# Layer 0's MLP: the first projection in seven products of quarters per pair of feature tiles

## The chip, the cores and the metric

The kernel runs on one core of a Trainium2 chip. A core has TensorE (PE, the matmuls; its weight loads stand in a row of their own, PEld), VectorE (DVE), ScalarE (ACT), GpSimd (POOL) and SyncE (SP), which here issues all the DMAs. The metric is the device time of one execution in microseconds (us). The kernel before takes 1741.64 us (median of 3 runs, 1736.88 to 1743.53).

## The reference

A block of two layers works on 512 latent tokens and 256 context tokens of width 1024. Each layer is a token mixer (layer 0: gated linear attention, "GLA"; layer 1: neighbourhood attention, "NA") and then a gated MLP with a depthwise convolution of width 3 over the tokens. Each of these four parts starts with an RMS norm that is scaled and shifted by vectors computed from the conditioning input (adaLN: six vectors of 1024 per layer), and ends with a gate and a residual add. What the change touches is the MLP and the adaLN vectors:

```
mod_l = (sc_lat @ ada_w[i] + ada_b[i])[:, None, :]          # six vectors per layer: shift, scale, gate, twice

def conv_ffn(h, w_in, conv_w, conv_b, w_out):               # D_MODEL 1024, D_FF 2816
    a, val = jnp.split(h @ w_in, 2, axis=-1)
    ap = jnp.pad(a, ((0, 0), (1, 1), (0, 0)))
    a = ap[:, :-2] * conv_w[0] + ap[:, 1:-1] * conv_w[1] + ap[:, 2:] * conv_w[2] + conv_b
    return (jax.nn.silu(a) * val) @ w_out
```

In layer 0 the MLP runs on the context tokens too (768 tokens in all), in layer 1 on the 512 latent ones alone. All arithmetic is float32.

## The kernel before, in words

Activations are kept transposed: features on the 128 partitions, tokens along the free axis. `H` holds the normed input of a projection as two float32r tiles, `hh` (the rounded value) and `hl` (what the rounding left); weights are held the same way as `wh` and `wl`. A product of full accuracy is then three matmuls, in `mm3` (L249 `hh` by `wl`, L250 `hl` by `wh`, L251 `hh` by `wh`). The helper `wunit` brings a weight unit of 128x1024: a DMA into `st` (pool `wst`, 3 buffers), an ACT copy into `wh` (L244), a DVE subtraction into `wl` (L245; pool `whl`, 5 buffers of each).

The stages run in this order: start and first norm, GLA, the GLA's output projection with the second norm (`finish_gla`), layer 0's MLP, NA, layer 1's MLP with the final norm. A static scheduler lays out the program: it sets the order of the instructions on each engine when the kernel is built, and each engine then works through its own list strictly in that order, waiting where an operand is late.

Layer 0's MLP has 22 pairs of feature tiles j (a tile of `a` and a tile of `val`, 128 features each), in six groups of three and a last group of four. For each pair, `in_tile` makes four matmul groups of 8 k-blocks x 3 matmuls: for `a` the 512 latent tokens (LAT) and the 256 context tokens (CTX), then the same for `val`. `finish` then does, on one row of 769 columns: ACT copies the `a` results into `apad` (L788), DVE convolves (L822, L823, L824), ACT applies Silu (L825), DVE multiplies by `val` (L830) and splits the result into `uh` and `ul` (L261 ACT, L262 DVE). After a group of three pairs comes the second projection: for each of 8 output tiles and both token ranges, 9 matmuls over the group's three tiles, and a gated add into the residual on DVE (L273). I call the two halves of a group its **in-phase** and its **out-phase**.

Between the pairs, DVE also computes eight adaLN vectors of layer 1 (`ada_lanes`): per vector eight DMAs of 512 KB into `sa` (pool `ast`, 2 buffers) and eight DVE multiply-adds of 128x1024 into `acc` (L201, L203), four steps after each pair; PE then sums over the partitions.

NA works through eight pairs of heads. For one pair, PE projects the next pair's q, k and v, makes scores (L964), transposes the softmax'd scores (`turn`, L989) and multiplies them with v (`values`, L1006). Between them DVE adds the bias and takes the maximum (L971), POOL, ACT and DVE do the softmax, and ACT (L992) and DVE (L994) each copy one head's transposed scores `PT` out of PSUM, which `values` waits for.

## Time and profile before

| | |
|---|---|
| median of 3 runs | 1741.64 us (1736.88 to 1743.53) |
| the profiled execution, its own time | 1739.42 us |
| its span, first to last instruction | 1737.6 us |
| mean granted TensorE clock in it | 0.993 |
| PE, PEld, DVE, ACT, POOL busy | 97%, 81%, 62%, 38%, 11% of the span |
| layer 0's MLP, in the trace | from about 452 us to about 1020 us |
| NA, in the trace | from about 1040 us to about 1345 us |

How to read the views that follow. The page gives the busy time of each engine over the span and the chain of work that ended last. A row that groups instructions reads: line, engine, operation, tile written from tiles read, shapes, count, then busy us in total, mean ns of one, and after the bar the idle time of the engine before them with what ended it. A timeline row reads: start us, duration us, engine, line, operation. A matmul's duration contains the time to run through the array, so that the rows of consecutive matmuls overlap: what a matmul costs is the distance between two starts. A row of stretches reads: stretch, its length, then for each engine busy us and, in brackets, the number of instructions.

### The profile page before, as it was taken

What the parts mean: (1) busy time and instruction counts of PE and PEld (TensorE: products, weight loads), DVE (VectorE), ACT (ScalarE), POOL (GpSimd) and SP (SyncE); (2) the same over time, 40 slices, a digit from 0 to 9 for tenths busy, and PEclk for the clock granted to TensorE, in tenths of its full rate; (3) what the DMA queues carried; (4) which work ended last, traced back from release to release, by engine and by line L of the source; (5) the groups of instructions that cost most, each with busy time, mean ns of one, the idle gap of its engine ahead of it and who ended that gap; (6) DMA issues with size and microseconds to landing.
All of it is one profiled execution on the core that took longest, in us unless ns stands there. A gap on an engine that the chain in (4) does not pass through costs nothing.

```text
span 1737.6 us, 27175 instructions
## 1 busy us (share of the span) xinstructions
PE 1681.7 (97%) x11107; PEld 1413.8 (81%) x11107; DVE 1070.4 (62%) x1699; ACT 658.7 (38%) x1173; POOL 190.9 (11%) x324
## 2 busy tenths in 40 slices
PE   5999999999999999999999999999999999999997
PEld 3767778778888888888888888888888888888887
DVE  4797777977666655656544575445456755555555
ACT  3675655653422121212213264443334522222332
POOL 1031212220000000000000015332222000000000
PEclk9999999999999999999999999999999999999999
DMA  7553423026224543544412122112111233223321
GB/s 274 173 171 122 154 90 104 19 72 220 86 73 152 160 125 110 179 147 146 122 60 86 49 68 79 54 42 66 54 56 42 75 97 98 90 82 95 109 85 49
DMA packets 54188, 179.70 MB, mean 103 GB/s; under 512 B 7024, under 2 KB 10864, under 8 KB 54064
## 3 DMA queue, kind: packets, MB, share of 16 engines
q1 hardware_dynamic: 54064, 177.97, 32.6%
q8 instruction: 87, 1.43, 0.3%
q14 instruction: 37, 0.30, 0.1%
HBM read 173.75 MB, written 2.10 MB: 101 GB/s over the span
## 4 chain that ended last, share of the span: by engine, by line
PE 80%; DVE 10%; ACT 4%; DMA 2%; issue 2%; POOL 1%; SPq 0%; POOLq 0%; DVEq 0%; ACTq 0%
PE mm L249 18%; PE mm L251 17%; PE mm L250 17%; PE aux L249 6%; PE aux L250 6%; PE aux L251 6%; PE mm L1006 2%; DMA sa<-in 2%; PE aux L989 2%; PE aux L964 2%; DVE t L526 1%; PE aux L605 1%; PE aux L570 1%; DVE acc L203 1%; DVE t L525 1%
## 5 line engine op out<-in xcount | busy, mean ns | idle before, releaser
L249 PE MATMUL mm<-hh,wl 128*128 128x512 f32 (+3 forms) x1104 | 388.6, 354 | 3.9 <-ACT hh L329 2.5
L251 PE MATMUL mm<-hh,wh 128*128 128x512 f32 (+3 forms) x1104 | 383.3, 348 | 0.0
L250 PE MATMUL mm<-hl,wh 128*128 128x512 f32 (+3 forms) x1104 | 383.0, 347 | 0.0
L244 ACT ACTIVATE wh<-st 128x1024 fp32r<-128x1024 f32 (+1 forms) x189 | 196.2, 1052 | 314.1 <-PE mm L251 162.4
L245 DVE TENSOR_TENSOR wl<-st,wh 128x1024 fp32r<-128x1024 f32 (+1 forms) x188 | 229.1, 1228 | 32.3 <-ACT wh L244 31.7
L249 PEld LDWEIGHTS mm<-hh,wl 128*128 128x128 f32 (+1 forms) x1104 | 208.8, 190 | 35.8 <-issue 5.5
L250 PEld LDWEIGHTS mm<-hl,wh 128*128 128x128 f32 (+1 forms) x1104 | 209.4, 190 | 24.3 <-issue 0.8
L251 PEld LDWEIGHTS mm<-hh,wh 128*128 128x128 f32 (+1 forms) x1104 | 209.1, 189 | 24.4 <-issue 0.4
L249 PE MATMUL aux<-hh,wl 128*128 128x512 f32 (+2 forms) x576 | 201.1, 349 | 0.0
L250 PE MATMUL aux<-hl,wh 128*128 128x512 f32 (+2 forms) x576 | 201.0, 349 | 0.0
L251 PE MATMUL aux<-hh,wh 128*128 128x512 f32 (+2 forms) x576 | 200.8, 349 | 0.0
L249 PE MATMUL mm<-uh,wl 128*128 128x512 f32 (+1 forms) x560 | 194.1, 350 | 1.7 <-ACT uh L261 1.4
L250 PE MATMUL mm<-ul,wh 128*128 128x512 f32 (+1 forms) x560 | 194.2, 348 | 0.0
L251 PE MATMUL mm<-uh,wh 128*128 128x512 f32 (+1 forms) x560 | 193.3, 346 | 0.0
L273 DVE SCALAR_TENSOR_TENSOR xl<-mm,mod,xl 128x512 f32<-128x512 f32 (+1 forms) x168 | 116.3, 698 | 108.9 <-PE mm L251 108.6
L305 POOL TENSOR_TENSOR rs<-ms,mhalf 128x2 f32<-128x2 f32 (+1 forms) x10 | 11.6, 1160 | 1036.6 <-DVE ms L303 1036.6
L249 PEld LDWEIGHTS mm<-uh,wl 128*128 128x128 f32 x560 | 105.8, 190 | 20.0 <-ACT uh L261 3.7
L249 PEld LDWEIGHTS aux<-hh,wl 128*128 128x128 f32 x576 | 109.2, 190 | 15.0 <-issue 1.4
L250 PEld LDWEIGHTS aux<-hl,wh 128*128 128x128 f32 x576 | 109.2, 190 | 14.4 <-issue 1.1
L251 PEld LDWEIGHTS aux<-hh,wh 128*128 128x128 f32 x576 | 109.1, 189 | 14.0 <-issue 0.8
L250 PEld LDWEIGHTS mm<-ul,wh 128*128 128x128 f32 x560 | 106.4, 190 | 14.3 <-DVE ul L262 0.3
L251 PEld LDWEIGHTS mm<-uh,wh 128*128 128x128 f32 x560 | 106.2, 190 | 13.1
(207 smaller groups left out, 2462.4 us busy)
## 6 DMA issues: line engine op xcount, KB each, us to landing
st<-in SPq DMA_DIRECT2D x201, 512.0 KB, 3.7
sa<-in SPq DMA_DIRECT2D x98, 512.0 KB, 4.3
sx<-in SPq DMA_DIRECT2D x14, 512.0 KB, 5.7
xl<-in SPq DMA_DIRECT2D x8, 512.0 KB, 5.6
xc<-in SPq DMA_DIRECT2D x4, 512.0 KB, 7.8
out<-y SPq DMA_DIRECT2D x16, 128.0 KB, 1.7
raw<-in SPq DMA_DIRECT2D x16, 96.0 KB, 2.4
t<-q SPq DMA_DIRECT2D x16, 64.0 KB, 2.0
```

The lines of the kernel that those rows point to most:

```text
L203: nc.vector.scalar_tensor_tensor(acc[0], st, cs[:, k, c:c + 1], acc[0], OP.mult, OP.add)
L244: nc.scalar.activation(hi, st, AF.Copy)
L245: (eng or nc.vector).tensor_sub(lo, st, hi.bitcast(F32))
L249: mm(out, a[1], b[0], start=first, stop=False)
L250: mm(out, a[0], b[1], start=False, stop=False)
L251: mm(out, a[0], b[0], start=False, stop=last)
L273: nc.vector.scalar_tensor_tensor(x_, ps, gate(l, n, d, rng), x_, OP.mult, OP.add)
L525: nc.vector.tensor_mul(eq, eq, st[h]["q"])
L526: nc.vector.tensor_mul(ek, ek, st[h]["k"])
L964: mm(pss[hh][:, off:off + 256], qe[a_][p_, 128 * t:128 * t + 128], ke[b_][p_, ks], start=i == 0, stop=i == 2)
L989: nc.tensor.transpose(pT[:, i * 128:(i + 1) * 128], S2[:, o:o + 128], ident)
L1006: mm(po[64 * hh:64 * hh + 64, 128 * t:128 * t + 128], V[:, vs[i], 64 * hh:64 * hh + 64], PTs[hh][:, i * 128:(i + 1) * 128], start=i == 0, ...
```

## The change

The first projection of layer 0's MLP is done, for pairs j = 2 to 21, by a scheme of seven products in place of eight (Winograd's form of Strassen's). The 2x2 block matrix on one side is [`a` weights; `val` weights] by halves of the contraction (k-blocks 0 to 3 and 4 to 7); on the other side it is the input by halves of the contraction and by halves of the tokens (0 to 383, 384 to 767). Each product is 4 k-blocks x 3 matmuls of 128x384. Three sums of input quarters (`T2`, `T3`, `T4`) are made once (`sums`); for that the norm keeps its result in float32 (`keep=R`). Four sums of weight halves (`S1` to `S4`) are made for every pair on DVE, and each of the seven weight halves is split into `wh` and `wl`. Two partial results are accumulated on in PSUM after ACT has copied the state so far (`copied`), and DVE adds put the parts together (`to_pad`, L930, L935). The convolution's first step moves from DVE to ACT (L773). Pairs 0 and 1 are done as before (`plain`).

All weights, in every stage, now come, are split and are released by halves of 128x512 (`wload`, `wsplit`; pools of 6 and 10). The adaLN vectors m = 2 to 5 of layer 1 are computed in the NA stage, one step of 128x1024 at four places of each pair of heads; m = 0 and 1 stay in the MLP, two steps per pair of tiles, each as two multiply-adds of 128x512. PE's part of such a vector is 8 matmuls against a vector of ones.

```diff
-    wst = ctx.enter_context(tc.tile_pool(name="wst", bufs=3))
+    wst = ctx.enter_context(tc.tile_pool(name="wst", bufs=6))
-    whl = ctx.enter_context(tc.tile_pool(name="whl", bufs=5))
+    whl = ctx.enter_context(tc.tile_pool(name="whl", bufs=10))
...
+    def wload(src):
+        st = wst.tile([128, 512], F32, name="st", tag="st")
         nc.sync.dma_start(st, src)
+        return st
+
+    def wsplit(st, eng=None, scale=None):
+        hi = whl.tile([128, 512], FR, name="wh", tag="wh")
+        lo = whl.tile([128, 512], FR, name="wl", tag="wl")
+        if scale is None:
+            nc.scalar.activation(hi, st, AF.Copy)
+            (eng or nc.vector).tensor_sub(lo, st, hi.bitcast(F32))
+        else:
+            nc.scalar.activation(hi, st, AF.Copy, scale=scale)
+            nc.vector.scalar_tensor_tensor(lo, st, scale, hi.bitcast(F32), OP.mult, OP.subtract)
         return hi, lo
 
-    def mm3(out, a, b, first, last):
...
+            if self.keep:
+                t = self.keep[k][:, a:b]
+                nc.vector.scalar_tensor_tensor(t, xk(k, self.rng), a_, self.rb, OP.mult, OP.mult)
+                nc.scalar.activation(t, t, AF.Identity, bias=b_)
+                split_to(hi, lo, t)
+                return
...
+            def sums(k):
+
+
+                a, b = slice(0, HT), slice(HT, T)
+                r, q = R[k], R[k + 4]
+                nc.vector.tensor_sub(r[:, a], r[:, b], r[:, a])
+                nc.vector.tensor_sub(r[:, b], q[:, b], r[:, b])
+                nc.vector.tensor_sub(q[:, b], q[:, b], r[:, a])
+                nc.vector.tensor_sub(q[:, a], q[:, a], q[:, b])
+                for i, src in ((2, q[:, b]), (4, q[:, a]), (3, r[:, b])):
+                    split_to(TT[i][0][:, k, :], TT[i][1][:, k, :], src)
+
+            def quarter(i, k):
+
...
+            def product(ps, w, i, first):
+                for k in range(4):
+                    mm3(ps[:, 0:HT], tuple(t_[:, k * 128:k * 128 + 128] for t_ in w), quarter(i, k), first and k == 0,
+                        k == 3, skip_group_check=True)
+
...
+            def weights_a(j):
+                s_ = st[j] = {}
+                s_["a"] = [wload(w_fi[0, j, 0][:, 512 * i:512 * i + 512]) for i in range(2)]
+                s_["A"] = [wsplit(t_) for t_ in s_["a"]]
+
+            def weights_b(j):
+                s_ = st[j]
+                a0, a1 = s_["a"]
+                v0, v1 = (wload(w_fi[0, j, 1][:, 512 * i:512 * i + 512]) for i in range(2))
+                s1 = wst.tile([128, 512], F32, name="st", tag="st")
+                nc.vector.tensor_add(s1, v0, v1)
+                nc.vector.tensor_sub(v0, a0, v0)
+                nc.vector.tensor_sub(a0, s1, a0)
+                s_["S2"] = wsplit(a0)
+                s_["S1"] = wsplit(s1)
+                s_["S3"] = wsplit(v0)
+                s_["A22"] = wsplit(v1)
+                nc.vector.tensor_sub(a1, a1, a0)
+                s_["S4"] = wsplit(a1)
+
+            def first(j):
+                s_ = st[j]
+                s_["b1"], s_["b2"] = ps_aux(), ps_mm()
+                product(s_["b1"], s_["A"][0], 11, True)
+                s_["s1"] = copied(s_["b1"])
+                product(s_["b2"], s_["A"][1], 21, True)
+
+            def to_pad(j):
+                b2, s1 = st[j]["b2"], st[j]["s1"]
+                nc.vector.tensor_add(apad[:, 1:257], b2[:, 0:256], s1[:, 0:256])
+                nc.vector.tensor_add(apad[:, 258:386], b2[:, 256:HT], s1[:, 256:HT])
+
+            def middle(j):
+                s_ = st[j]
+                s_["b5"] = ps_aux()
+                product(s_["b1"], s_["S2"], 2, False)
+                s_["u2"] = copied(s_["b1"])
+                product(s_["b5"], s_["S1"], 12, True)
+                product(s_["b1"], s_["S3"], 3, False)
+                s_["u3"] = copied(s_["b1"])
+                nc.vector.tensor_add(s_["u3"], s_["b5"][:, 0:HT], s_["u3"])
...
+            def final_(j):
+                s_ = st[j]
+                product(s_["b5"], s_["S4"], 22, False)
+                nc.vector.tensor_add(apad[:, 386:770], s_["b5"][:, 0:HT], s_["u2"])
+                product(s_["b1"], s_["A22"], 4, False)
+                b1 = s_["b1"]
+                u = finish(j, [(0, 256, b1[:, 0:256]), (256, HT, b1[:, 256:HT]), (HT, T, s_["u3"])])
+                for job in jobs[:2]:
+                    job()
+                del jobs[:2]
+                return u
+            jobs = []
+            for m, c in ((0, 0), (0, 1), (1, 0), (1, 1)):
+                jobs += ada_lanes(lambda: [whl.tile([128, 512], F32, name="acc", tag=tg) for tg in ("wh", "wl")], 1, m,
+                                  c)
...
+            for grp in GROUPS:
+                for j in grp:
+                    if j < 2:
+                        continue
+                    if j < NF - 1:
+                        weights_a(j + 1)
+                        first(j + 1)
+                    us[j] = final_(j)
+                    if j < NF - 1:
+                        to_pad(j + 1)
+                        weights_b(j + 1)
+                        middle(j + 1)
+                ul = [us[j] for j in grp]
+                if grp is GROUPS[-1]:
+                    w = [wunit(w_fo[0, j]) for j in grp]
+                    last_outs(0, [w_.blk for w_ in w], ul, 0, (LAT, CTX),
+                              lambda rng: Norm(pool, 1, 0, rng, blocks=rng == LAT, tag="tt", sq=(whl, "wl"),
...
             for d in range(2 * t0, 2 * t1):
                 out_group(m, d)
 
+        jobs = []
+        for m in range(2, 6):
+            jobs += ada_lanes(lambda: [pool.tile([128, D], F32, name="acc", tag="acc", bufs=1)], 1, m, 0)
...
+            jobs.pop(0)()
             turn(pr, 0)
             scores(pr, 2)
+            jobs.pop(0)()
             values(pr, 0)
...
```

How the order of instructions moves, at three places. First PE, in the in-phase of a pair, where one matmul group ends and the next begins (names: output tile, then the moving and the stationary operand). Before, the end of `a`'s latent tokens and the start of its context tokens:

```order
L249 MATMUL mm_7583<-hh_126,wl_7580 128x512
L250 MATMUL mm_7583<-hl_127,wh_7579 128x512
L251 MATMUL mm_7583<-hh_126,wh_7579 128x512
L249 MATMUL mm_7609<-hh_126,wl_7580 128x256
L250 MATMUL mm_7609<-hl_127,wh_7579 128x256
L251 MATMUL mm_7609<-hh_126,wh_7579 128x256
```

Now, the end of the product with `S2` into the first accumulator and the start of the product with `S1` into the other:

```order
L250 MATMUL aux_7921<-T2h_4379,wl_8005 128x384
L251 MATMUL aux_7921<-T2l_4380,wh_8004 128x384
L252 MATMUL aux_7921<-T2h_4379,wh_8004 128x384
L250 MATMUL aux_8025<-hh_123,wl_8009 128x384
L251 MATMUL aux_8025<-hl_124,wh_8008 128x384
L252 MATMUL aux_8025<-hh_123,wh_8008 128x384
```

Groups of 24 matmuls of 512 and of 256 columns have become products of 12 matmuls of 384 columns, with a weight half of its own each.

Second DVE, in the middle of an in-phase. Before, the work around one pair's convolution (`acc` is an adaLN step, `wl` a weight split, L822 to L830 the convolution and the product with `val`):

```order
L822 TENSOR_SCALAR tt<-apad_4765,sT 128x769
L203 SCALAR_TENSOR_TENSOR acc<-sa,cs,acc 128x1024
L823 SCALAR_TENSOR_TENSOR tt<-apad_4765,sT,tt 128x769
L245 TENSOR_TENSOR wl<-st,wh 128x1024
L824 SCALAR_TENSOR_TENSOR tt<-apad_4765,sT,tt 128x769
L203 SCALAR_TENSOR_TENSOR acc<-sa,cs,acc 128x1024
L830 TENSOR_TENSOR u<-tt,aux 128x512
L203 SCALAR_TENSOR_TENSOR acc<-sa,cs,acc 128x1024
L830 TENSOR_TENSOR u<-tt,aux 128x256
L245 TENSOR_TENSOR wl<-st,wh 128x1024
L262 TENSOR_TENSOR ul<-u,uh 128x768
L203 SCALAR_TENSOR_TENSOR acc<-sa,cs,acc 128x1024
```

Now, the same place (L774 and L775 are the convolution, L919 and L920 `to_pad`, L856 the product with `val`, L930 the join of two partial results, `wl` a split of a weight half):

```order
L240 TENSOR_TENSOR wl<-st,wh 128x512
L775 SCALAR_TENSOR_TENSOR tt<-apad,sT,tt 128x769
L919 TENSOR_TENSOR apad<-mm,cp 128x256
L920 TENSOR_TENSOR apad<-mm,cp 128x128
L856 TENSOR_TENSOR tt<-tt,aux 128x256
L856 TENSOR_TENSOR tt<-tt,aux 128x128
L240 TENSOR_TENSOR wl<-st,wh 128x512
L856 TENSOR_TENSOR tt<-tt,cp 128x384
L240 TENSOR_TENSOR wl<-st,wh 128x512
L263 TENSOR_TENSOR ul<-tt,uh 128x768
L930 TENSOR_TENSOR cp<-aux,cp 128x384
L240 TENSOR_TENSOR wl<-st,wh 128x512
```

The adds that join partial results stand between the steps of the convolution, and the splits have half the size and stand one by one among them.

Third DVE in NA, between the projection of one pair of heads and the scores of the next (L971, now L1129: bias and maximum; L994, now L1152: the copy of `PT` that `values` waits for). Before:

```order
L994 COPY PT<-aux 128x512
L952 COPY V<-aux 128x512
L245 TENSOR_TENSOR wl<-st,wh 128x1024
L994 COPY PT<-aux 128x512
L971 ISA S_10475,mx<-aux,bias_9445 128x512
L971 ISA mx 128x1
L971 ISA S_10475,mx<-aux,bias_9446 128x512
L971 ISA mx 128x1
L978 RECIPROCAL ri<-sm 128x1 x2
L262 TENSOR_TENSOR ol<-mm,oh 128x7x8x8
L262 TENSOR_TENSOR ol<-mm,oh 128x8x8
```

Now:

```order
L1110 COPY V<-aux 128x512
L198 TENSOR_SCALAR acc<-sa,cs 128x1024
L240 TENSOR_TENSOR wl<-st,wh 128x512
L1152 COPY PT<-aux 128x512
L200 SCALAR_TENSOR_TENSOR acc<-sa,cs,acc 128x1024
L1129 ISA S_11350,mx<-aux,bias_10213 128x512
L1129 ISA mx 128x1
L1129 ISA S_11350,mx<-aux,bias_10214 128x512
L1129 ISA mx 128x1
L263 TENSOR_TENSOR ol<-mm,oh 128x7x8x8
L1136 RECIPROCAL ri<-sm 128x1
L200 SCALAR_TENSOR_TENSOR acc<-sa,cs,acc 128x1024
```

Steps of an adaLN vector (L198, L200) stand between the copies of `PT` and around the bias and maximum of the next scores.

More of the change, by code (lines that the diff above doesn't have):

```diff
@@ L206, in step @@
             ps = ps_aux()
[L207 to L214 removed]
+            for d in range(KD):
+                a_ = acc[d * 128 // n]
+                o = d * 128 % n
+                mm(ps[:, 2 * d:2 * d + 2], a_[:, o:o + 128], ones, start=True, stop=True)
             o = 8 * m
             mod = modT[l][:, o:o + 8, c]
[L217 to L220 removed]
+            nc.vector.tensor_add(mod, ps[:, 0:16:2], sT[:, R_AB + 48 * l + o:R_AB + 48 * l + o + 8])
             if m in (1, 4):
@@ L348, in start_weights @@
         def start_weights(i, src, eng=None):
-            w = tuple(w.rearrange("p (k n) -> p k n", k=KD) for w in wunit(src, eng=eng))
-            groups[2 * i][0] = groups[2 * i + 1][0] = w
+            w = wunit(src, eng=eng)
+            n = src.shape[-1] // KD
+            groups[2 * i][0] = groups[2 * i + 1][0] = w.blk if n == 128 else lambda k: tuple(
+                t_[:, n * k:n * k + n] for t_ in w.halves[0])
         start_weights(0, a_w1)
@@ L752, in finish_gla @@
         return todo + cx.steps()
-    def ffn(l, after):
-        first = 0 if l == 0 else 2
-        seqs = ((0, 256), (256, 768)) if l == 0 else ((256, 768),)
-        rngs = (LAT, CTX) if l == 0 else (LAT,)
-        base = seqs[0][0]
-        n_tok = 768 - base
-        n_pad = n_tok + len(seqs) + 1
-        def pad_of(tok):
-            return tok - base + 1 + (1 if len(seqs) == 2 and tok >= 256 else 0)
-        with tc.tile_pool(name=f"ffn{l}", bufs=4) as pool:
-            left = finish_gla(pool) if l == 0 else []
-            apad = [pool.tile([128, n_pad], F32, name=f"apad{i}", tag=f"apad{i}", bufs=1) for i in range(2)]
-            edges = [0, n_pad - 1] + ([257] if len(seqs) == 2 else [])
+    GROUPS = [tuple(range(3 * g, 3 * g + 3)) for g in range(6)] + [(18, 19, 20, 21)]
@@ new lines, in conv @@
+    def conv(l, j, tt, ap_):
+        cw = [sT[:, R_CW + l * 66 + tap * 22 + j:R_CW + l * 66 + tap * 22 + j + 1] for tap in range(3)]
+        cb = sT[:, R_CB + l * 22 + j:R_CB + l * 22 + j + 1]
+        m = tt.shape[1]
+        if l:
+            nc.vector.tensor_scalar(tt, ap_[:, 1:1 + m], cw[1], cb, OP.mult, OP.add)
+        else:
+            nc.scalar.activation(tt, ap_[:, 1:1 + m], AF.Identity, bias=cb, scale=cw[1])
+        nc.vector.scalar_tensor_tensor(tt, ap_[:, 0:m], cw[0], tt, OP.mult, OP.add)
+        nc.vector.scalar_tensor_tensor(tt, ap_[:, 2:2 + m], cw[2], tt, OP.mult, OP.add)
+        nc.scalar.activation(tt, tt, AF.Silu)
@@ new lines, in ffn_out, with last_outs @@
+    def ffn_out(ws, us, d, rng, base):
+        a, b = rng
+        ps = ps_mm()[:, 0:b - a]
+        for i, (w, u) in enumerate(zip(ws, us)):
+            mm3(ps, w(d), (u[0][:, a - base:b - base], u[1][:, a - base:b - base]), i == 0, i == len(us) - 1)
+        return ps
+    def last_outs(l, ws, us, base, rngs, norm_of):
+        todo = []
+        for rng in rngs:
+            norm = norm_of(rng)
+            for d in range(KD):
+                ps = ffn_out(ws, us, d, rng, base)
+                if todo:
+                    todo.pop(0)()
+                add_gated(ps, l, 1, d, rng)
+                norm.add(d)
+            todo += norm.steps()
+        for f in todo:
+            f()
@@ L770, in ffn, with ffn1 @@
+    def ffn1(after):
+        n_tok = N_LAT
+        with tc.tile_pool(name="ffn1", bufs=4) as pool:
+            apad = [pool.tile([128, n_tok + 2], F32, name=f"apad{i}", tag=f"apad{i}", bufs=1) for i in range(2)]
             for ap_ in apad:
-                for e in edges:
+                for e in (0, n_tok + 1):
                     nc.gpsimd.memset(ap_[:, e:e + 1], 0.0)
-            def pieces(a, b):
-                return [(max(a, s0), min(b, s1)) for s0, s1 in seqs if max(a, s0) < min(b, s1)]
@@ L777, in in_weights @@
-            def in_weights(j, which):
-                return tuple(w.rearrange("p (k n) -> p k n", k=KD) for w in wunit(w_fi[l, j, which]))
             def in_group(j, which, w, rng):
@@ L909, in weights @@
         def weights(pr, i):
-            sp[pr]["w", i] = tuple(w.rearrange("p (k n) -> p k n", k=KD) for w in wunit(w_nqk[pr, i]))
+            sp[pr]["w", i] = wunit(w_nqk[pr, i])
         def proj(pr, i, rng):
@@ L1093, in body @@
         todo = []
+        nacc = pool.tile([128, D], F32, name="nacc", tag="acc", bufs=1)
         for a, b in ((0, 256), (256, 512)):
-            norm = Norm(pool, 1, 1, (N_CTX + a, N_CTX + b))
+            norm = Norm(pool, 1, 1, (N_CTX + a, N_CTX + b), acc=nacc[:, a:b])
             for d in range(KD):
```

280 lines of the change are left out of this document (144 added, 136 removed).

## The prediction

> **What bounds the kernel now.** I read the page first, the engines' busy time and the chain that ended last:
>
> ```profile
> PE 1681.7 (97%) x11107; PEld 1413.8 (81%) x11107; DVE 1070.4 (62%) x1699; ACT 658.7 (38%) x1173; POOL 190.9 (11%) x324
> PE 80%; DVE 10%; ACT 4%; DMA 2%; issue 2%; POOL 1%; SPq 0%; POOLq 0%; DVEq 0%; ACTq 0%
> ```
>
> PE is busy nearly all the time and carries 80% of the chain. An average says little about one stage, so I asked for two stretches, one whole group of three pairs in layer 0's MLP and most of NA, and for PE's waits from the second norm to the start of NA (385 to 1045 us):
>
> ```profile
> 526.20:601.80 75.60, 75.60 (x442) 65.40 (x441) 50.85 (x60) 16.86 (x23) 0.00 (x0) 1.00 0.55 174
> 1045.00:1345.00 300.00, 298.90 (x2219) 249.83 (x2219) 155.46 (x350) 122.54 (x258) 95.04 (x190) 1.00 0.18 54
> ```
> ```profile
> PE aux L308 <- POOL rs L305: 3.8, 4, 1.2
> PE mm L249 <- ACT uh L261: 1.4, 2, 1.2
> ```
>
> The busy columns are PE, PEld, DVE, ACT, POOL. In the MLP PE never pauses: its waits over 660 us are a few us. DVE works 50.85 of 75.60 us, so a third of it is free. The granted clock is 1.00. A matmul taken away here is therefore worth its whole distance to the next one, as long as DVE can keep up with the work that replaces it.
>
> That distance I take from starts on PE's timeline, for 512 columns, for 256, and, from the GLA stage, for 384:
>
> ```profile
> 703.94 0.39 PE L249 MATMUL mm<-hh,wl 128*128 128x512 f32 x1
> 704.17 0.39 PE L250 MATMUL mm<-hl,wh 128*128 128x512 f32 x1
> 704.39 0.39 PE L251 MATMUL mm<-hh,wh 128*128 128x512 f32 x1
> ...
> 706.05 0.28 PE L249 MATMUL mm<-hh,wl 128*128 128x256 f32 x1
> 706.17 0.28 PE L250 MATMUL mm<-hl,wh 128*128 128x256 f32 x1
> ```
> ```profile
> 209.25 0.33 PE L249 MATMUL mm<-hh,wl 128*128 128x384 f32 x1
> ...
> 212.19 0.34 PE L251 MATMUL mm<-hh,wh 128*128 128x384 f32 x1
> ```
>
> 512 columns cost 0.2275 us and 256 cost 0.120. Between the two quoted rows of 384 lie 17 distances: 2.94 / 17 = 0.173 us, on the straight line between the other two. So 384 columns pay no penalty, although a weight load per matmul stays.
>
> **The change part by part.**
>
> *The products.* A pair took 48 matmuls of 512 and 48 of 256: 48 x 0.2275 + 48 x 0.120 = 16.68 us. Now it takes 7 x 12 = 84 of 384: 84 x 0.173 = 14.53 us, or 2.15 less. Twenty pairs: **-43.0 us**. The second projection keeps its 72 matmuls per range and group, 72 x (0.2275 + 0.120) = 25.0 us per out-phase.
>
> *What DVE must do for it.* Prices of one operation:
>
> ```profile
> L245 DVE TENSOR_TENSOR wl<-st,wh 128x1024 fp32r<-128x1024 f32 x187 | 228.4, 1231 | 32.3 <-ACT wh L244 31.7
> L262 DVE TENSOR_TENSOR ul<-u,uh 128x512 fp32r<-128x512 f32 x22 | 15.1, 685 | 1.4 <-ACT uh L261 1.4
> L262 DVE TENSOR_TENSOR hl<-aux,hh 128x384 fp32r<-128x384 f32 x12 | 6.0, 546 | 0.0
> L294 DVE TENSOR_TENSOR nacc<-nacc,sq 128x256 f32<-128x256 f32 x49 | 20.8, 424 | 5.1 <-ACT sq L293 3.9
> L262 DVE TENSOR_TENSOR ul<-u,uh 128x768 fp32r<-128x768 f32 x22 | 20.9, 952 | 0.9 <-ACT uh L261 0.9
> L823 DVE SCALAR_TENSOR_TENSOR tt<-apad,sT,tt 128x769 f32<-128x769 f32 x22 | 22.4, 1020 | 0.6
> L273 DVE SCALAR_TENSOR_TENSOR xl<-mm,mod,xl 128x512 f32<-128x512 f32 x136 | 101.1, 749 | 108.2 <-PE mm L251 108.0
> ```
>
> In the new order one in-phase (between the gated adds of two out-phases, pairs 12 to 14) holds 75 DVE instructions: 32 of 512 columns at 0.685 (23 splits, six of them of weights for the second projection, and 9 sums), 8 multiply-adds of 512 at 0.749, 6 of 769 at 1.02, 9 of 384 at 0.546, 6 of 256 at 0.424, 3 of 768 at 0.952, and small ones, 3.6 together. That is 21.9 + 6.0 + 6.1 + 4.9 + 2.5 + 2.9 + 3.6 = 47.9 us, against 3 x 14.53 = 43.6 us on PE. End to end it would not fit. But instructions on DVE overlap:
>
> ```profile
> 803.53 0.68 DVE L822 TENSOR_SCALAR tt<-apad,sT 128x769 f32<-128x769 f32 x1
> 804.12 1.28 DVE L203 SCALAR_TENSOR_TENSOR acc<-sa,cs,acc 128x1024 f32<-128x1024 f32 x1
> 805.31 1.02 DVE L823 SCALAR_TENSOR_TENSOR tt<-apad,sT,tt 128x769 f32<-128x769 f32 x1
> 806.24 1.22 DVE L245 TENSOR_TENSOR wl<-st,wh 128x1024 fp32r<-128x1024 f32 x1
> ```
>
> Each starts 0.09 us before the one ahead has ended (803.53 + 0.68 = 804.21, start 804.12). 75 x 0.085 = 6.4 us less: 41.5 us. I walked through this in-phase by hand in DVE's new order, each instruction at its duration less 0.085, ACT's Silu, copy and the convolution's first step at 0.85 each, and a product's result when PE has reached it. DVE waits 1.7 us for the first `S4` product (PE has it at 6.2 us) and about a microsecond per pair for ACT; the three pairs' `ul` are done 15.2, 29.5 and 44.1 us after the out-phase's end, so DVE needs some 14.5 us a pair, as PE does. PE starts the next out-phase at 43.6 us, does two tiles of it (6 x 0.2275) and needs `ul` at 45.0. The cover is there, with 1 us of slack. PE's queue holds the whole next out-phase behind that wait. What can eat the slack is DMA: the slot for a `val` half comes free only when another half has been split, and adaLN steps wait for theirs:
>
> ```profile
> DVE acc L203 <- DMA sa<-in: 26.0, 23, 3.5
> st<-in SPq DMA_DIRECT2D x201, 512.0 KB, 3.7
> ```
>
> (Waits from 470 to 985 us: 26.0 us over 23 times; then the landing time of a weight unit.) A wait of 1.1 us is the mean, so I take 0.8 us of PE time lost per group, for six groups **+5**; from 0 to 2.5 us a group (+15), which is what the walk gives without the overlap. In the out-phase DVE has 28 instructions, 18.6 us, in 25.0.
>
> *The start of the MLP.* Between the last gated add of the second norm and the first of an out-phase DVE now has 114 instructions, 68.7 us end to end by the same rows, 59.0 with the overlap: 16 sums and 16 splits of 384 for the quarters and `hl`, the norm's context part, 38 splits and sums of weight halves, three convolutions. PE has pairs 0 and 1 (33.4), pair 2 (14.53) and five sevenths of pair 3 (10.4): 58.3 us. The first split stands behind the last gated add, 1.2 us, and the third `uh`/`ul` ends about 2 us behind PE. I take **+3**, from 0 to +11 (no overlap).
>
> *NA.* 32 steps of 1.28 us (0.75 for a vector's first) are 39 us of DVE in a stage where it is busy 155 of 300. Their weak place is between `turn` and `values`:
>
> ```profile
> 1067.58 0.87 PE aux L989 x8
> 1068.45 0.91 PE aux L964 x12
> 1069.36 1.02 PE mm L1006 x16
> ...
> L994 DVE COPY PT<-aux 128x512 f32<-128x512 f32 x32 | 22.1, 691 | 34.9 <-PE aux L989 34.5
> L203 DVE SCALAR_TENSOR_TENSOR acc<-sa,cs,acc 128x1024 f32<-128x1024 f32 x56 | 71.8, 1282 | 29.4 <-DMA sa<-in 29.3
> ```
>
> PE's chain runs from the transposes through 0.91 us of scores to `values`, which needs a copy of 0.69: next to no slack at that place, 32 times; elsewhere a projection (24 x 0.2275 = 5.5 us) covers. The copy itself waits for PE 34.9 / 32 = 1.1 us each, into which a step of 1.2 fits nearly. In the new order a step stands directly ahead of a copy in about one case of four; 8 x 0.7 is **+6**; 0 if all fall into the idle time, +15 if the DMA's waits add to half of them. Behind a late copy PE holds `values` and everything after.
>
> *The rest.* Weight halves: 2 x (0.685 - 0.085) against 1.231 - 0.085 is 0.05 us more DVE and some 200 more DMA issues on SP, all behind work that is there now; only GLA, where DVE is in the chain, can feel it. The last norm of the MLP has two temporaries instead of four. Together **+2**, from -1 to +6. PE's part of an adaLN vector stays about 1 us, moved rather than saved: 0.
>
> [...]
>
> **Sum:** -43.0 + 5 + 3 + 6 + 2 = -27 us. The profiled execution took 1739.4 (span 1737.6), which gives 1712.4; the median shown is 2.2 above it, so I forecast **1714 us**.
>
> **The rivals.**
>
> 1. *All cover holds*: no stall in groups, start or NA: 1741.6 - 43 + 1 = 1700. For it: DVE fits on paper everywhere. Against: six hand-overs with 1 us of slack, each behind DMAs.
>
> 2. *DVE becomes the bound of the in-phases*: its instructions run end to end where they depend on each other through ACT. Then the group's last `ul` comes at 47.6 us, PE waits 2.5 us in six groups (+15) and the start costs +11: -43 + 15 + 11 + 6 + 2 = -9, or 1733. The timeline's overlap speaks against it, yet the in-phase would have DVE over 90% busy, which no row of before shows for 40 us. [...]
>
> 3. *Slower: the adaLN steps in NA.* SP's list is in order; a step's DMA behind a weight half that waits for a slot comes late, DVE stands at the step, and the softmax and `PT` copies stand behind it. Price: 1.28 of the step and 1.1 of DMA wait, 32 x 2.4 = 77 us at most, with the rest as forecast 1741.6 - 33 + 77 = 1786. It decides from 33 us, or 1.0 us per step on PE's path. For it: PE never waits in NA now, so any delay shows. Against: 145 us of idle DVE there, and steps one at a time rather than four in a row. Half of its price gives 1747.
>
> That the change does less on PE than it says I give no chance: 84 for 96 matmuls stand in the order.
>
> **How the numbers follow.** The forecast has 0.62 (by itself 1703 to 1727), rival 1 0.13, rival 2 0.17, rival 3 0.08. The likeliest is 1714. The range takes in rivals 1 and 2: 1697 to 1737. About 0.5% (8.7 us) is what a measurement of this kernel can tell from no change, so faster means below 1733: the forecast, rival 1 and over half of rival 2, 0.84; same: the rest of rival 2, 0.08; slower 0.08.
>
> **What would show it.** Right: the period of a group falls from 75.6 to about 70 us; matmuls of 384 start 0.173 us apart; DVE is 54 to 59 us busy per group (66.5 end to end, less 103 overlaps); PE waits for `uh` or `ul` once a group, under 2 us; NA takes 305 to 312 us between the places that are 300 apart now. Wrong: PE waits for split weights inside a pair, or a group's period above 73 us (rival 2); `values` waiting for `PT` dozens of times with DVE at adaLN steps (rival 3); a DVE list held for several us by `sa` or `st` DMAs, which would show the slots of halves as the bound.

## The result, and the profile after

The changed kernel takes 1754.15 us (median of 4 runs, 1751.31 to 1755.34) against 1739.57 us for the kernel before (median of 4): a ratio of 1.008, with a 95% interval from 1.0054 to 1.0106. It is slower by some 14 us, where 27 us less were forecast. Its profiled execution took 1754.39 us (span 1752.5, mean granted clock 0.983). One execution of a kernel further below, sq_own_2, took 2324.87 us at a granted clock of 0.655 and is left out of that kernel's figures. The page of after begins:

```profile
PE 1666.9 (95%) x10915; PEld 1433.8 (82%) x10915; DVE 1220.3 (70%) x2168; ACT 769.9 (44%) x1487; POOL 199.3 (11%) x320
PE 75%; DVE 13%; ACT 4%; DMA 3%; issue 3%; POOL 2%; SPq 0%; POOLq 0%; DVEq 0%; ACTq 0%
```

PE's busy time fell by 14.8 us, and DVE's share of the chain rose from 10% to 13%. To see where the time went I cut both traces at the same events: the first and the last gated add of GLA's output projection, the first gated add of the first and of the last out-phase, and the first and the last scores of NA. On DVE's timeline, of before and then of after:

```profile
391.61 0.75 DVE L273 SCALAR_TENSOR_TENSOR xl<-mm,mod,xl 128x512 f32<-128x512 f32 x1
450.11 0.49 DVE L273 SCALAR_TENSOR_TENSOR xc<-mm,mod,xc 128x256 f32<-128x256 f32 x1
505.14 0.75 DVE L273 SCALAR_TENSOR_TENSOR xl<-mm,mod,xl 128x512 f32<-128x512 f32 x1 [0.84 <-PE mm L251]
```
```profile
397.39 0.75 DVE L274 SCALAR_TENSOR_TENSOR xl<-mm,mod,xl 128x512 f32<-128x512 f32 x1 [1.11 <-PE mm L252]
487.80 0.48 DVE L274 SCALAR_TENSOR_TENSOR xc<-mm,mod,xc 128x256 f32<-128x256 f32 x1 [4.36 <-PE mm L252]
551.88 0.74 DVE L274 SCALAR_TENSOR_TENSOR xl<-mm,mod,xl 128x512 f32<-128x512 f32 x1
984.08 2.07 DVE L274 SCALAR_TENSOR_TENSOR xl<-mm,mod,xl 128x512 f32<-128x512 f32 x3 [0.83 <-PE mm L252]
```

The last group's first gated add starts at 984.08 in both kernels; in before it is a single one, in after three stand there in a row. For NA the row of the first scores matmul gives both ends (count, shortest, median and longest in ns, first and last start), before and after:

```profile
L964 PE MATMUL aux<-kh,ql x128: 275/333/385, 1045.3 to 1327.3; 64*128 64x256 f32 x128
```
```profile
L1122 PE MATMUL aux<-kh,ql x128: 274/332/579, 1048.6 to 1341.0; 64*128 64x256 f32 x128
```

The stages of the two kernels, and of three experiments that are told below, in us:

| stage | before | after | sq_own_1 | before_sq_in_pool | mlp_rows_in_sa |
|---|---|---|---|---|---|
| start and GLA | 391.6 | 397.4 | 395.0 | 394.9 | 394.9 |
| GLA's output projection | 58.5 | 90.4 | 55.7 | 92.0 | 55.7 |
| start of the MLP | 55.0 | 64.1 | 62.9 | 58.4 | 64.4 |
| groups of the MLP | 479.0 | 432.2 | 433.4 | 478.2 | 434.5 |
| last outputs to NA's scores | 61.2 | 64.5 | 65.1 | 60.0 | 66.2 |
| NA | 282.0 | 292.4 | 290.7 | 282.0 | 282.7 |
| the rest | 410.3 | 411.5 | 412.5 | 410.5 | 408.2 |
| span | 1737.6 | 1752.5 | 1715.3 | 1776.0 | 1706.6 |

In after, 8.3 us of the start's 64.1 are work that the new program does ahead (five sevenths of pair 3, less what pair 2 saves), and the groups are shorter by as much. So by this cut the groups won 46.8 - 8.3 = 38.5 us (the account of the prediction below cuts them on PE, which gives more), and one stage, which the change hardly seems to touch, lost 31.9: GLA's output projection. The stretches of that stage, before and after (the columns as in the prediction: length, then PE, PEld, DVE, ACT, POOL, granted clock, DMA):

```profile
391.60:450.10 58.50, 57.37 (x344) 51.74 (x343) 45.48 (x68) 26.60 (x42) 1.45 (x1) 0.97 0.64 198
```
```profile
397.40:487.80 90.40, 68.92 (x338) 56.29 (x336) 39.76 (x66) 31.52 (x53) 1.11 (x2) 0.89 0.25 86
```

PE is idle for 21.5 us in place of 1.1, and the same matmuls keep it busy for 68.9 us in place of 57.4, at a granted clock of 0.89: 20.4 and 11.5 us make up the 31.9. No engine is full there; DVE works 39.8 of 90.4 us. It is a stage in which all wait for each other. The waits of after in this stretch, and a piece of DVE's timeline in it:

```profile
PE mm L250 <- DVE wl L243: 20.9, 17, 2.8
```
```profile
409.27 0.75 DVE L274 SCALAR_TENSOR_TENSOR xl<-mm,mod,xl 128x512 f32<-128x512 f32 x1 [6.31 <-PE mm L252]
409.94 0.74 DVE L243 SCALAR_TENSOR_TENSOR wl<-st,sT,wh 128x512 fp32r<-128x512 f32 x1
410.72 0.69 DVE L298 TENSOR_TENSOR apad<-apad,sq 128x512 f32<-128x512 f32 x1
411.33 0.74 DVE L243 SCALAR_TENSOR_TENSOR wl<-st,sT,wh 128x512 fp32r<-128x512 f32 x1
418.84 0.75 DVE L274 SCALAR_TENSOR_TENSOR xl<-mm,mod,xl 128x512 f32<-128x512 f32 x1 [6.76 <-PE mm L252]
```

For each output tile DVE adds the last one (L274), splits the two weight halves of the next (L243), and then stands still for 6.8 us until PE has used them. ACT waits too, 19.7 us in this stretch, for loads into `st`. The first tiles take 9.6 us each, where 24 matmuls are worth 5.5 (24 x 0.2275). The same piece of before shows units split far ahead, five splits between two gated adds (the next one is at 399.29):

```profile
394.04 0.75 DVE L273 SCALAR_TENSOR_TENSOR xl<-mm,mod,xl 128x512 f32<-128x512 f32 x1
394.70 0.69 DVE L294 TENSOR_TENSOR nacc<-nacc,sq 128x512 f32<-128x512 f32 x1
395.30 1.41 DVE L242 SCALAR_TENSOR_TENSOR wl<-st,sT,wh 128x512 fp32r<-128x512 f32 x2
396.62 0.69 DVE L294 TENSOR_TENSOR nacc<-nacc,sq 128x512 f32<-128x512 f32 x1
397.23 2.08 DVE L242 SCALAR_TENSOR_TENSOR wl<-st,sT,wh 128x512 fp32r<-128x512 f32 x3
```

One line of the change can do that: `finish_gla(pool, acc=apad[:, 0:T], sq=(whl, "wl"), keep=R)`. The squares of the second norm, which were in a pool of their own (`t2`), take slots of `wl`, the tag of the weights' rounding parts in their pool `whl`. In DVE's list the splits of a tile then stand behind the gated add that the square ahead of them in the program needs: 409.94 behind 409.27 in the rows above. It is hardly the number of slots: a tile takes three of the ten (two halves and a square), so three tiles would fit.

### The profile page after: what moved, and what is told of

Same layout as the page of the kernel before. It is cut to its first block, busy times and chain, and to the rows that moved or that the text cites. A ratio compares the mean times of both kernels' runs of the same rounds, so it can differ in the third digit from the quotient of the medians.

```text
span 1752.5 us, 28205 instructions
## 1 busy us (share of the span) xinstructions
PE 1666.9 (95%) x10915; PEld 1433.8 (82%) x10915; DVE 1220.3 (70%) x2168; ACT 769.9 (44%) x1487; POOL 199.3 (11%) x320
## 3 DMA queue, kind: packets, MB, share of 16 engines
q1 hardware_dynamic: 83008, 177.99, 31.9%
## 4 chain that ended last, share of the span: by engine, by line
PE 75%; DVE 13%; ACT 4%; DMA 3%; issue 3%; POOL 2%; SPq 0%; POOLq 0%; DVEq 0%; ACTq 0%
PE mm L250 15%; PE mm L251 14%; PE mm L252 14%; PE aux L250 7%; PE aux L251 7%; PE aux L252 7%; DMA sa<-in 2%; PE mm L1164 2%; PE aux L1147 1%; DVE wl L240 1%; PE aux L1122 1%; PE aux L612 1%; PE aux L577 1%; DVE t L533 1%; DMA st<-in 1%
## 5 line engine op out<-in xcount | busy, mean ns | idle before, releaser
L239 ACT ACTIVATE wh<-st 128x512 fp32r<-128x512 f32 x437 | 269.0, 627 | 397.1 <-PE mm L252 271.6
L240 DVE TENSOR_TENSOR wl<-st,wh 128x512 fp32r<-128x512 f32 x435 | 300.6, 700 | 79.7 <-ACT wh L239 75.2
L250 PE MATMUL mm<-hh,wl 128*128 128x512 f32 (+3 forms) x864 | 313.7, 365 | 28.2 <-DVE wl L243 20.9
L251 PE MATMUL mm<-hl,wh 128*128 128x512 f32 (+3 forms) x864 | 306.9, 356 | 0.0
L252 PE MATMUL mm<-hh,wh 128*128 128x512 f32 (+3 forms) x864 | 305.9, 355 | 0.0
L250 PEld LDWEIGHTS mm<-hh,wl 128*128 128x128 f32 (+1 forms) x864 | 166.0, 193 | 57.9 <-DVE wl L243 27.1
L274 DVE SCALAR_TENSOR_TENSOR xl<-mm,mod,xl 128x512 f32<-128x512 f32 (+1 forms) x168 | 116.7, 697 | 111.7 <-PE mm L252 110.2
L251 PEld LDWEIGHTS mm<-hl,wh 128*128 128x128 f32 (+1 forms) x864 | 167.0, 193 | 17.4 <-issue 0.4
L250 PE MATMUL aux<-hh,wl 128*128 128x384 f32 (+2 forms) x496 | 174.0, 351 | 0.0
L251 PE MATMUL aux<-hl,wh 128*128 128x384 f32 (+2 forms) x496 | 173.8, 350 | 0.0
L252 PE MATMUL aux<-hh,wh 128*128 128x384 f32 (+2 forms) x496 | 173.6, 350 | 0.0
```

Of the source, the lines that this page charges most:

```text
L239: nc.scalar.activation(hi, st, AF.Copy)
L240: (eng or nc.vector).tensor_sub(lo, st, hi.bitcast(F32))
L250: mm(out, a[1], b[0], start=first, stop=False, **at)
L251: mm(out, a[0], b[1], start=False, stop=False, **at)
L252: mm(out, a[0], b[0], start=False, stop=last, **at)
L274: nc.vector.scalar_tensor_tensor(x_, ps, gate(l, n, d, rng), x_, OP.mult, OP.add)
```

## The experiments

Of each edit I show the lines that matter; `...` stands for the others.

**Squares out of the weight pool.** The memory of `T2` and `T3` is free until the sums of quarters are made; the squares go there.

```diff
-            left = finish_gla(pool, acc=apad[:, 0:T], sq=(whl, "wl"), keep=R)
+            tags = ["T2h", "T2l", "T3h", "T3l"] * 4
+            left = finish_gla(pool, acc=apad[:, 0:T], keep=R,
+                              sq=lambda: pool.tile([128, 512], F32, name="sq", tag=tags.pop(0), bufs=1))
...
```

> The changed kernel, with one difference: the squares of the second norm (in `finish_gla`) are written to memory of `T2` and `T3`, which is still free there, and no longer to slots of the weight pool (tag `wl`). Theory A, shared slots: a weight half's `wl` can only take its slot behind the squares that stand ahead of it in the program, and these wait for gated adds, so each output tile loads, splits and multiplies in turn. Then the first gated add of the first out-phase comes at 521 to 527 us in place of 551.9 (before: 505.1; what stays is 8 us of work done ahead, GLA's +6 and about +3 at the MLP's start), PE's waits for `wl` in that stage fall from 20.9 to under 3 us, and the time falls by 24 to 31, to 1723 to 1731. Theory B, the halves themselves: loads and splits of 128x512 cost the stage its cover; the waits stay, and the time stays above 1747. Theory C, the kept norm (the normed input kept in float32) makes DVE the bound there: above 1747 too, with DVE busy throughout.

Measured: 1717.83 us, ratio 0.9866 (0.9851 to 0.9881). One line is worth 36 us. The stage takes 55.7 us, PE waits for no `wl` in it, and the list looks ahead again:

```profile
397.66 0.75 DVE L274 SCALAR_TENSOR_TENSOR xl<-mm,mod,xl 128x512 f32<-128x512 f32 x1
398.32 0.68 DVE L300 TENSOR_TENSOR apad<-apad,sq 128x512 f32<-128x512 f32 x1
398.92 1.41 DVE L243 SCALAR_TENSOR_TENSOR wl<-st,sT,wh 128x512 fp32r<-128x512 f32 x2
400.25 0.69 DVE L300 TENSOR_TENSOR apad<-apad,sq 128x512 f32<-128x512 f32 x1
```
```profile
395.00:450.70 55.70, 54.84 (x341) 49.49 (x341) 38.25 (x65) 28.74 (x52) 1.56 (x2) 1.00 0.37 124
```

The halves and the kept norm are still in this kernel, so theories B and C fall. The gain is larger than expected: the first gated add of the first out-phase comes at 513.6, not at 521 or later.

**The same step alone, in the kernel before.**

```diff
-        lat, cx = Norm(pool, 0, 1, LAT), Norm(pool, 0, 1, CTX)
+        lat, cx = (Norm(pool, 0, 1, rng, sq=lambda n=rng[1] - rng[0]: whl.tile([128, 1024], F32, name="sq", tag="wl")[:, 0:n])
+                   for rng in (LAT, CTX))
...
```

> The kernel before, with one difference: the squares of the second norm take slots of the weight pool (tag `wl`, whole units). Nothing else of the change is in it. Theory A: GLA's output projection slows in the same way; PE waits for `wl` there for 10 to 25 us and the time rises by 12 to 32, to 1752 to 1772. Theories B and C: no change, 1737 to 1744.

Measured: 1777.63 us, ratio 1.0211 (1.0194 to 1.0228): 37 us slower, above the range expected. The stage takes 92.0 us, with the same waits and a clock of 0.87, though weights come as whole units and nothing else of the change is there:

```profile
PE mm L249 <- DVE wl L242: 21.2, 16, 3.5
```
```profile
394.90:486.90 92.00, 70.04 (x338) 58.15 (x336) 47.47 (x72) 25.71 (x41) 1.01 (x1) 0.87 0.35 122
```

Taken out of one kernel and put into the other, the shared slots alone give the loss. That settles the main cause.

**Weights by halves alone.** The kernel before with `wload`, `wsplit` and `W` of the change in every stage.

```diff
-    wst = ctx.enter_context(tc.tile_pool(name="wst", bufs=3))
-    whl = ctx.enter_context(tc.tile_pool(name="whl", bufs=5))
+    wst = ctx.enter_context(tc.tile_pool(name="wst", bufs=6))
+    whl = ctx.enter_context(tc.tile_pool(name="whl", bufs=10))
...
```

> The kernel before, with all weights loaded, split and released by halves (pools of 6 and 10), squares and adaLN as before. Theory A: halves are cheap wherever PE is the bound; only GLA, where ACT and DVE stand in the chain, pays some 6 us (its first gated add at 397 in place of 391.6): +3 to +9, 1743 to 1749. Theory B: the output projection shows the waits for `wl` and takes 25 us or more longer: above 1764. Theory C: 0 to +6.

Measured: 1747.98 us, ratio 1.0046 (1.0031 to 1.0061). Nearly all of it comes before the output projection: its first gated add is at 399.5 us, 7.9 later than before, and every later stage is as long as before within 3.5 us (57.1, 55.0, 482.4, 60.3, 282.6, 409.6). So halves alone don't slow the output projection, and they cost no later stage more than these 3.5 us. How much they cost GLA is not shown: in the other kernels with halves the same add comes between 394.0 and 397.5, and in before_sq_in_pool, which has whole units, at 394.9. What in GLA is late I did not follow further.

**Squares at the end of the MLP out of the pool too.** Before NA the same line stands once more, in `last_outs`, and PE waits 6.8 us there:

```profile
1020.40 0.99 PE L305 MATMUL aux<-ones,apad 128*128 128x2 f32 x4 [6.81 <-DVE apad L298]
```

```diff
-                              lambda rng: Norm(pool, 1, 0, rng, blocks=rng == LAT, tag="tt", sq=(whl, "wl"),
-                                               acc=apad[:, rng[0]:rng[1]]))
+                              lambda rng: Norm(pool, 1, 0, rng, blocks=rng == LAT, tag="tt", acc=apad[:, rng[0]:rng[1]],
+                                               sq=lambda: pool.tile([128, 512], F32, name="sq", tag=tags.pop(0),
+                                                                    bufs=1)))
...
```

> As sq_own_1, and the squares of the next norm, at the end of layer 0's MLP, are taken out of the weight pool too (memory of `T3` and `T4`). Theory A: the 6.8 us in which PE waits for the context part's sum of squares at 1013 us, and the 3.4 us that the lower granted clock costs behind it (0.83 over 20 us), come from NA's first weights being split behind those squares, so that PE has no projection to do meanwhile: a further 4 to 10 us less than sq_own_1, 1714 to 1726. Rival: DVE is simply behind there, with two temporaries for the norm's apply in place of four; then the wait stays and the time is within 2 us of sq_own_1.

Measured: 1719.4 us, ratio 0.9879 (0.9863 to 0.9896): nothing won on sq_own_1. The wait of 6.8 us is gone, and from the last group's first gated add to NA's first scores the time falls from 65.1 to 62.1. But NA takes 296.3 in place of 290.7, with new waits at its start (995 to 1045 us):

```profile
PE mm L250 <- ACT v L1092: 3.7, 1, 3.7
PE mm L1170 <- DVE PT L1158: 1.6, 1, 1.6
PE mm L1170 <- ACT PT L1156: 1.4, 1, 1.4
```

DVE waits there for `sa`, 3.9 us once, so the adaLN steps are suspects. To move them away from NA's start, the first of the four vectors went into the MLP and the others behind the second pair of heads:

```diff
-            for m, c in ((0, 0), (0, 1), (1, 0), (1, 1)):
+            for m, c in ((0, 0), (0, 1), (1, 0), (1, 1), (2, 0)):
...
-        for m in range(2, 6):
+        for m in range(3, 6):
...
-            jobs.pop(0)()
+            if pr >= 2:
+                jobs.pop(0)()
...
```

> As sq_own_2, but of the four adaLN vectors of NA the first (m = 2) is computed in layer 0's MLP, in the eight places that are free there, and the other three from the third pair of heads on. Theory: the steps in the first two pairs stand in DVE's list where it is busiest (18 of 20 us) and hold it for late DMAs (3.9 us once), so PE waits for DVE and ACT and runs at a lower clock. Then from the last group's first gated add to NA's first scores 58 to 61 us in place of 62.1, NA 287 to 291 in place of 296.3, and 1711 to 1716 in all. Rival: the start of NA is late for the norm's own work; then 1718 to 1722.

Measured: 1720.99 us, ratio 0.9903 (0.9885 to 0.9921), and NA 297.7. But the edit did not do all that it says: the scheduler put steps at the start of NA all the same, and one of them held DVE's list for a DMA:

```profile
1020.88 1.28 DVE L200 SCALAR_TENSOR_TENSOR acc<-sa,cs,acc 128x1024 f32<-128x1024 f32 x1 [6.27 <-DMA sa<-in]
```

So this kernel says nothing on the theory; mlp_rows_in_sa_sq_2 below does.

**The sums over the partitions.** In after, PE's part of an adaLN vector is 16 matmuls of 2 columns; in before it was 8 matmuls and two transposes (float32 matmuls of these lines stand twice in the trace: the programs have 8 and 4). After first:

```profile
1115.46 1.84 PE L207 MATMUL aux<-ones,acc 128*128 128x2 f32 x16
1117.17 0.64 PE L1109 MATMUL aux<-ident,v 128*128 128x128 f32 x4
```
```profile
543.00 0.64 PE L208 MATMUL aux<-acc,one 128*32 128x256 f32 x8
543.57 0.50 PE L249 MATMUL mm<-hh,wl 128*128 128x512 f32 x1
...
545.53 0.38 PE L214 MATMUL aux<-ident,rows 128*128 128x128 f32 x2
```

From start to start that is 1.7 us against 0.57 and some 0.2. With the old form for NA's four vectors:

```diff
-            for d in range(KD):
...
+            if one_row:
+                one0, rows = one_row[0], one_row[1]()
+                for j in range(4):
+                    mm(ps[32 * j:32 * j + 32, 0:256], one0, acc[0][:, 256 * j:256 * j + 256], start=True, stop=True,
+                       skip_group_check=True)
+                nc.scalar.activation(rows, ps[:, 0:256], AF.Copy)
+                pm = ps_aux()
+                for f in range(2):
+                    nc.tensor.transpose(pm[:, f * 128:(f + 1) * 128], rows[:, f * 128:(f + 1) * 128], ident)
...
+            for d in range(0 if one_row else KD):
...
```

> As sq_own_1, but PE's part of the four adaLN vectors of the NA stage is done as in the kernel before: 4 matmuls of 256 columns and two transposes (0.66 and 0.24 us in the trace of before) in place of 16 matmuls of 2 columns (1.7 us). Theory: that is all that most of NA's 8.7 us are, 4 x 0.8 = 3 us of it: from the first to the last scores 287.5 us in place of 290.7 (before: 282.0), and 1713 to 1716 in all. Rival: the steps on DVE are what costs, by late copies of `PT`; then nothing changes (290 to 291, 1717 to 1719).

Measured: 1711.82 us, ratio 0.9852 (0.9831 to 0.9873); NA takes 288.6 us in place of 290.7. Eight kernels of this record with no adaLN step in NA take 282.0 to 282.7 us there, so these 2 us are clear of the spread: they are the form of the sum. With the old form a vector still costs PE its time there. The two edits in one kernel:

> ada_late and row_sums in one kernel: 3 vectors x 0.8 = 2.4 us less than ada_late, 1709 to 1714 in all. It holds everything found so far, and should beat the kernel before by 1.5 to 1.8%.

Measured: 1716.81 us, ratio 0.9879 (0.9863 to 0.9895): 4 us less than ada_late, with much the same waits at NA's start, and 1.2% below the kernel before in place of the 1.5 to 1.8% expected.

**All vectors back in the MLP.** This asks how much room DVE has in an in-phase.

```diff
-                for job in jobs[:2]:
+                for job in jobs[:4]:
...
-            for m, c in ((0, 0), (0, 1), (1, 0), (1, 1)):
+            for m, c in ((0, 0), (0, 1), (1, 0), (1, 1), (2, 0), (3, 0), (4, 0), (5, 0)):
...
```

> As sq_own_1, but all eight adaLN vectors are computed in layer 0's MLP, four steps after each pair of tiles, and none in NA. Theory (the prediction's): DVE has next to no room in an in-phase, so that two more steps, 4 operations of 512 columns at 0.75 - 0.085 = 2.7 us, make a pair longer by some 2 us, 16 times: a group takes 75 to 78 us in place of 70.8, NA is 8.7 us shorter, and the time is 1733 to 1745. Rival: DVE still has room (it is busy 38.9 of 47.5 us in an in-phase of sq_own_1): a group takes 72 us (two sums of 1.7 us more in some), and the time is 1710 to 1720.

Measured: 1714.17 us, ratio 0.9863 (0.9846 to 0.988). NA takes 282.6 us, as before, and a group 72.1 in the mean. The period of a group, with DVE at 62.9 of 72.7 us:

```profile
660.60:733.30 72.70, 72.70 (x428) 69.43 (x427) 62.89 (x109) 27.34 (x45) 0.00 (x0) 1.00 0.47 145
```

PE waits for `uh` and `ul` for 0.7 us in all seven groups together. The rival is right: DVE had room for two more steps per pair. The next kernel adds the cheaper sums in the MLP, with the temporary `rows` in a slot of the weight pool:

```diff
+            rows = whl.tile([128, 512], F32, name="rows", tag="wh")[:, 0:256]
...
```

> As ada_in_mlp, with PE's part of all eight vectors as rows of 256 columns and two transposes, in place of 16 matmuls of 2 columns. By row_sums a vector is then 0.5 to 0.8 us cheaper: a group takes 71.0 us in place of 72.1, and the time falls by 4 to 6.5, to 1707.5 to 1710.

Measured: 1755.93 us, ratio 1.0095 (1.008 to 1.011): 42 us slower than ada_in_mlp, not 4 to 6.5 faster. I had made the mistake that I was studying. An in-phase with a vector's end in it takes up to 60.3 us, where ada_in_mlp needs 49.1, with these waits of PE (380 to 1340 us):

```profile
PE aux L257 <- DVE wl L247: 12.5, 8, 1.9
PE aux L206 <- DVE acc L200: 9.4, 6, 2.5
PE aux L212 <- ACT rows L209: 4.2, 8, 0.6
```

Three more kernels carried the same line, so their comparison with mlp_row_sums is all that they give. With sq_own_2's edit, the squares out of the pool before NA:

> As mlp_row_sums, with the squares at the end of layer 0's MLP out of the weight pool as in sq_own_2. There it brought nothing, since waits for ACT and DVE came at the start of NA. Theory: those came from the adaLN steps in NA's first pairs. They are gone here, so the 6.8 us of waiting before NA and the lower clock behind them are now won: 1698 to 1703. Rival: the norm's own work and NA's first splits fill DVE and ACT there; then within 3 us of mlp_row_sums.

Measured: 1753.92 us; to NA's first scores 62.3 us in place of 66.1, and NA stays at 282.6. Then the context's norm written behind NA's first projections, and the same with four buffers (memory of `T3` and `T4`) for the apply's temporary:

```diff
         for i in range(3):
             proj(0, i, LAT)
...
+        for f in late_norm[0].steps():
+            f()
...
```

> As mlp_row_sums, with the context part of the norm after layer 0's MLP (sum of squares, scale, apply) written behind NA's first three projections of the latent tokens, which don't need it. PE then has 3 x 24 x 0.2275 = 16.4 us of work between the last output tile and the context's sum of squares. Theory: no wait of 6.8 us there, no drop of the granted clock (0.74 over 20 us in sq_own_1, 5.2 us): 8 to 12 us less than mlp_row_sums, 1696 to 1701. Rival: DVE is the bound of this stretch, and the wait turns up at the first scores or projections of the context: within 3 us of it.

> As ctx_norm_later, with four buffers in place of two for the temporary of the latent part's apply (memory of `T3` and `T4`). Theory: two buffers hold ACT and DVE in turn there, so 1 to 4 us less than ctx_norm_later. Rival: they don't bound it, and the time is the same within 2 us.

Measured: 1754.19 and 1754.94 us. The wait before the context's sum of squares is there as before (6.7 us): the scheduler put the sum ahead of the projections again. Both are inconclusive on what the wait is worth.

**The slot, and only the slot.** `rows` takes a buffer of the adaLN loads.

```diff
-            rows = whl.tile([128, 512], F32, name="rows", tag="wh")[:, 0:256]
+            rows = ast.tile([128, 1024], F32, name="rows", tag="sa")[:, 0:256]
```

> As mlp_row_sums, but the 128x256 temporary of a vector's sum (`rows`) takes a buffer of the adaLN loads (tag `sa`) in place of one of the weight pool (tag `wh`). Theory, shared slots: in mlp_row_sums the weight halves that follow in the program got their place only behind `rows`, and this waits for the last adaLN step; so the 42 us that mlp_row_sums is above ada_in_mlp vanish, and the row sums' own gain shows: 1706 to 1711, groups of 71 to 72 us without waits of PE. Rival, the row sums themselves: PE waits for ACT's copy and DVE's last step in the middle of a pair, whatever memory they use; then 1745 or more.

> As mlp_rows_in_sa, with the squares at the end of layer 0's MLP out of the weight pool as in sq_own_2. Theory: sq_own_2 brought nothing because the adaLN steps at NA's start filled DVE; there are none here, so the 3 to 4 us that it gained up to NA's first scores are kept: 1702 to 1707, NA 282 to 284. Rival: the norm's own work and NA's first splits take them back: within 2 us of mlp_rows_in_sa.

Measured: 1707.25 us, ratio 0.9808 (0.9792 to 0.9823), and 1706.31 us, ratio 0.9809 (0.9784 to 0.9834). The first shows that in mlp_row_sums it was the slot again: 49 us from one tag. In the second the way to NA's first scores falls from 66.2 to 59.7 us and NA takes 282.6: the gain that sq_own_2 gave back is kept where no adaLN step stands in NA. In whole times the two can't be told apart. Either beats the kernel before by 33 us or more, and the changed kernel by 47.

## Why the prediction was wrong

By its own terms, from the stage table, with the 8.3 us of work ahead put back into the groups and with the two ends of the groups taken on PE, at the first matmuls of the first and of the last out-phase: 500.90 and 979.88 us before, 548.60 and 976.65 after. The rows of the last out-phase, before and then after:

```profile
979.88 0.40 PE L249 MATMUL mm<-uh,wl 128*128 128x512 f32 x1
```
```profile
976.65 0.39 PE L250 MATMUL mm<-uh,wl 128*128 128x512 f32 x1
```

In after another 0.7 us of this out-phase, three matmuls, run ahead of 976.65. So at the gated adds of 984.08 PE has done 4.2 us of the out-phase in before and 8.2 in after: the stage table counts 4 us of the last outputs as groups.

| term | predicted | measured |
|---|---|---|
| products, with the groups' stalls | -43 + 5 = -38 | -51.7 + 8.3 = -43.4 |
| start of the MLP | +3 | 10.0 - 8.3 = +1.7 |
| NA | +6 | +10.4 |
| the rest | +2 (-1 to +6) | 5.8 + 31.9 + 7.3 + 1.2 = +46.2 |
| sum | -27 | +14.9 |

*The products* came out as priced, at -43, and the stalls of +5 did not come: that the stage table shows -38.5, near the forecast of both together, is luck. Five periods of a group went from 386.3 to 353.0 us, 2.2 us per pair. In after PE is busy through a whole period, and DVE's load, 56 to 61 us in the five periods, is about what I had forecast (54 to 59 us):

```profile
622.84:692.12 69.28, 69.28 (x399) 66.01 (x398) 59.16 (x101) 26.95 (x44) 0.00 (x0) 1.00 0.40 128
```

My walk through an in-phase found DVE at 14.5 us a pair, as long as PE, with 1 us of slack. ada_in_mlp shows that it had room for some 2.7 us more per pair (four operations of 0.75 us, less overlaps of 0.085). Rival 2 is refuted, and with it my reason for believing that the adaLN steps had to leave the MLP.

*The rest* is the step that failed. It said that the halves lie "all behind work that is there now", and outside GLA that was nearly so (before_halves). But it had no term at all for the squares that change pools, though the call with `sq=(whl, "wl")` and the wider `Norm` are in the change. I counted the start of the MLP from the last gated add of the second norm, so the stage ahead of it was never worked out; I took it as it stood in before. sq_own_1 and before_sq_in_pool show 36 and 37 us for that line. The last paragraph of the prediction names "the slots of halves as the bound" as a way to be wrong; slots it was, but those that a norm takes, and in a stage that I did not look at. The 7.3 us of the last outputs hold PE's wait of 6.8 us before NA, at the second norm that takes such slots; sq_own_2 removes the wait and gains nothing in all; mlp_rows_in_sa_sq_2, with no adaLN step in NA, keeps 6.5 us at that place.

*NA* was mis-sized inside. Late `PT` copies, on which the +6 rested, cost 1.6 us; this is PE's one kind of wait between the first and the last scores:

```profile
PE mm L1164 <- DVE PT L1152: 1.6, 2, 1.0
```

PE's part of a vector, "about 1 us, moved rather than saved: 0", is 1.7 us, and three of the four end in this stage: 5.1 of the 10.4. The clock, 0.97 and 0.94 in two slices of 20 us (1100 to 1140), makes another 1.8; 1.9 us stay unexplained. Rival 3's mechanism, DVE's list held by an `sa` DMA, exists (3.54 us once in after, 6.27 in ada_late), but waits of more than 1 us stand at NA's start alone, and it does not decide here.

*The clock* had no term either: 11.5 of the 31.9 us are the same matmuls at a lower granted clock, 0.89 in place of 0.97.

## What to carry to other kernels

A temporary that is put into a pool on which lookahead rests takes more than memory: in these lists the tiles that follow it in the program came behind what it waits for, so its own waits became theirs. When a change moves a tile to another pool or tag, ask for each user of that pool what now stands ahead of it, and walk through that stage in the new lists, even if it computes the same as before. And where a stage has waits, price them with the slow matmuls that can follow: here 11.5 us beside 21.5 us in which PE was idle.
